# Two modulation vectors moved into the first feed-forward's second half, and an S5 input product with exchanged operands

## The chip, the cores and the metric

The kernel runs on one core of one Trainium2 chip. The metric is device time in microseconds (us) of one execution. Before the change three executions took 1390.58, 1391.0 and 1392.18 us; the median is 1391.0 us.

## The reference, cut to what matters

One inference step of a two-layer trunk (width 1024), for a prompt of 512 tokens and 8 samples of one token. All data are fp32. Layer 0 has an "even" mixer (gated linear attention beside RG-LRU), layer 1 an "odd" mixer (S5 beside HGRN2), and each mixer is followed by a SwiGLU feed-forward of inner width 2816. Every mixer and feed-forward is modulated from a condition vector:

```
mod = silu(c) @ w_ada[l] + b_ada[l]            # 6 vectors of 1024 for each layer
sh_m, sc_m, gt_m, sh_f, sc_f, gt_f = split(mod, 6)
h = x * (1 + sc_m) + sh_m;  x = LN(ALPHA*x + (1 + gt_m) * mixer(h))
h = x * (1 + sc_f) + sh_f;  x = LN(ALPHA*x + (1 + gt_f) * swiglu(h))
```

The two vectors that the change moves are sh_f and sc_f of layer 1, vectors 3 and 4: they are used right after the odd mixer. The S5 part of the odd mixer is evaluated in blocks of 8 tokens. For that, 32 groups of small matrices are prepared from parameters alone; one of them is, for each group g, a product of BA[g] (128 contraction rows by 128 columns, 8 powers by 16 inputs) with CS[g] (128 by 16 outputs).

## The kernel before, in words

**Order of the work.** The program goes through the even mixer, feed-forward 0 (lines 780 to 886, in two halves of 11 column blocks, `hb` 0 and 1), the odd mixer (from line 1647 on), feed-forward 1. Weights stream from DRAM in an order written out by hand, the list `plan` (lines 279 to 291). Each entry is one load of up to 1 MB into one of three raw buffers (`wraw`, line 45), issued on SP's queue at line 176. An entry that is a weight for the main products is used as one or two units of 128 columns; for each, `make` (line 181) has ACT cast it to fp32r (`whi`, line 199) and DVE subtract the remainder (`wlo`, line 110), and a raw buffer is free again when the remainder of its last unit is done. A main product (`mm3`, lines 231 to 241) takes 48 matmuls of 260 columns for 8 contraction blocks.

**The modulation entries.** An entry of kind "ada" holds two contraction blocks of w_ada for a vector of 1024, 1 MB. `ada_part` (line 319) does 8 plain fp32 matmuls with it, at four column positions of the array: the condition (128 by 32) is the stationary operand and 256 columns of the weight are the moving one (line 323). Four parts make a vector; then `ada_rows` (line 326) copies the sum to SBUF on ACT (`adasb`, line 328), transposes it with two matmuls (line 147) and adds the bias on DVE. The parts of a vector share one of the four PSUM buffers `mx`. `mix` puts "ada" entries between others: `FB` (vectors 1 and 2 of layer 1, 8 entries) in pairs into the second half of feed-forward 0, and `OA` (vectors 3 and 4, 8 entries) one by one among the 10 input-projection entries of the odd mixer, read from `od_in`.

**The odd mixer's start.** The layer norm at the end of feed-forward 0 is worked in two halves of the tokens (lines 660 to 770). The first five units of the input projection are worked for each half as it comes (`first_units`, matmuls of lines 816 to 818). Units 0 to 3 give `u`. They are copied by ACT into `ut` (line 1671), stored to DRAM (`Ud`, line 1675, and `Usd`, line 1695), and read back in another layout into `u8` (lines 1697 to 1699, ten loads of short runs), all of it on SP's queue. The S5 product `s5_in` (line 1716) needs the whole of `u8`. After it come the other units, the seven levels of HGRN2's chunk products (`level`, matmuls of lines 924 and 944, with DVE updating the operands between them), the S5 output and the output projection.

**S5's preparation.** `s5_prep` (from line 1440 on) runs as a side job in the first half of feed-forward 0: after each unit of the input projection it goes on by one step. Its last part goes through four chunks of 8 groups. DVE builds BA in three operations, eight matmuls transpose it (line 147), ACT copies that to `sb` (line 1615), which goes to DRAM; eight plain fp32 matmuls (line 1620) make the product with BA as the stationary operand and 16 columns of CS as the moving one; ACT copies it to `Mall` (line 1622). DVE's next work on this (CA and W of the same chunk, and BA of the next) takes buffers from a ring of four with the tag "W", so that it can wait for line 1620.

The order of the instructions on each engine is set when the program is built, by a scheduler that works with a simulated time line, priorities and free buffers; the engines then run it in order.

Of the kernel before, what the change touches and what calls it, by code (L numbers as in the profile page):

```python
# [7 lines left out]
F32 = mybir.dt.float32  # L8
# [28 lines left out]
OD_COLS = [0, 256, 1024, 1280, 512, 768, 1536, 1792, 2048, 2304]  # L37


def build(tc, I, O):  # L40
    nc = tc.nc
    V, S, G, T, SY = nc.vector, nc.scalar, nc.gpsimd, nc.tensor, nc.sync
    with ExitStack() as ctx:
        def pool(n, b=1, **k):
            return ctx.enter_context(tc.tile_pool(name=n, bufs=b, **k))
# [5 lines left out]
        tmp = pool("tmp", 6)  # L51
# [14 lines left out]
        def mx():  # L66
            return ps["M"].tile([128, 512], F32, tag="mx", name="mx")
# [41 lines left out]
        def tt(out, a, b, op):  # L109
            V.tensor_tensor(out=out, in0=a, in1=b, op=op)  # L110

        def add(out, a, b):
            tt(out, a, b, ALU.add)
# [16 lines left out]
        def bc(ap, shape):  # L130
            return ap.to_broadcast(shape)
# [13 lines left out]
        def transpose(out, in_, base=0):  # L145
            k = in_.shape[0]
            T.transpose(out, in_, ident[base:base + k, base:base + k])  # L147

        plan = []
# [94 lines left out]
        od_in, od_out = I["od_w_in"][0], I["od_w_out"][0]  # L244
# [3 lines left out]
        def p_ada(l, js):  # L248
            return [("ada", I["w_ada"][l], k0, 2, D * j, D, l) for j in js for k0 in range(0, 8, 2)]

        def p_cols(kind, src, cols):
            return [(kind, src, 0, 8, c, 256) for c in cols]

        def p_ffn(l, hb):
            r = []
            for c in range(0, 11, 2):
                n = min(2, 11 - c) * 128
                c0 = (11 * hb + c) * 128
                r.append(("fin", f_in[l], 0, 8, c0, n))
                r.append(("fin", f_in[l], 0, 8, DFF + c0, n))  # L260
            for cs in ((0,), (256,), (512, 768)) if hb else ((0,), (256,), (512,), (768,)):
                r += [("fout", f_out[l], 11 * hb + 8, 3, c0, 256) for c0 in cs]
                r += [("fout", f_out[l], 11 * hb, 8, c0, 256) for c0 in cs]
            return r

        def mix(main, ada, first=1, per=2):
            r = list(main[:first])
            rest = main[first:]
            done = 0
            for n, c in enumerate(rest):  # L270
                want = (n + 1) * (len(ada) // per) // len(rest) * per
                r += ada[done:want]
                done = want
                r.append(c)
            return r

        FA = p_ada(0, [5]) + p_ada(1, [0])
        FB = p_ada(1, [1, 2])
        OA = p_ada(1, [3, 4])
# [3 lines left out]
        plan += mix(p_cols("in", ev_in, EV_COLS), p_ada(0, range(2, 4)))  # L283
        plan += mix(p_cols("out", ev_out, (0, 256)), p_ada(0, [4])[:2], 1) + p_ada(0, [4])[2:] + p_cols("out", ev_out, (512, 768))
        plan += mix(p_ffn(0, 0)[:12], FA[:4], 3) + mix(p_ffn(0, 0)[12:], FA[4:])
        plan += mix(p_ffn(0, 1)[:-4], FB, 2) + p_ffn(0, 1)[-4:]
        plan += mix(p_cols("in", od_in, OD_COLS), OA, 0, 1)
        plan.append(("glu", I["od_s5_w_glu"][0], 0, 4, 0, 512))
        plan += p_cols("out", od_out, range(0, D, 256))
        plan += mix(p_ffn(1, 0)[:12], LA, 2, 1) + p_ffn(1, 0)[12:] + p_ffn(1, 1)  # L290
# [8 lines left out]
        h = (lambda k: hhi[:, k], lambda k: hlo[:, k])  # L299
# [9 lines left out]
        def ada_mm(p, r):  # L309
            for k in range(8):  # L310
                c = k % 4
                T.matmul(p[32 * c:32 * c + 32, 0:256], condT[:, k, :], r[:, k, :],
                         start=(k < 4), stop=(k >= 4), tile_position=(0, 32 * c), skip_group_check=True)
            sb = cst.tile([128, 256], F32, tag="adasb", name="adasb")
            S.copy(sb, p[:, 0:256])
            for b in range(2):
                T.matmul(p[:, 256 + 16 * b:256 + 16 * b + 9], sb[:, 128 * b:128 * b + 128], sel, start=True, stop=True)
            return p[:, 256:288].rearrange("p (c r) -> p c r", r=16)[:, :, 0:9]
# [54 lines left out]
        with tc.tile_pool(name="st", bufs=1, reuse_waits="tile") as st:  # L373
# [73 lines left out]
            for f in range(8):  # L447
# [5 lines left out]
                with tc.high_priority(offset=2 * HIGH):  # L453
                    q = ada_mm(mx(), r)
# [13 lines left out]
                for k in lag[f]:  # L468
                    for hf in range(2):
                        T.matmul(lrp[rows[hf], :HN], wl[:, k, :], h32s[k][:, hf], start=(k == 0),  # L470
                                 stop=(k == 7), tile_position=(0, 32 * hf), skip_group_check=True)
# [966 lines left out]
        def s5_prep(sp):  # L1438
            if True:
# [3 lines left out]
                def wt(nm, sh, parts=128):  # L1443
                    return sp.tile([parts] + sh, F32, tag="W", name=nm, bufs=4)
# [14 lines left out]
                for q in range(2):  # L1459
                    p = mx()  # L1460
# [11 lines left out]
                for n in range(2):  # L1472
                    p = mx()
# [122 lines left out]
                CS = tmp.tile([128, 32, 16], F32, tag="t2k", name="CS")  # L1596
                V.tensor_copy(CS[lo_], CT[0][lo_])
                ts1(CS[hi_], CT[1][hi_], -1.0, ALU.mult)
                Mall = wt("Mall", [512])
                for ch in range(4):  # L1600
                    gs = slice(8 * ch, 8 * ch + 8)
                    eb = lambda t: bc(t[:, :, gs].rearrange("p e g -> p g e").unsqueeze(3), [128, 8, 8, 16])
                    BA = wt("BA", [8, 8, 16])
                    W = wt("W", [8, 8, 16])
                    bb_ = lambda t: bc(t[:, :, gs].rearrange("p h g -> p g h").unsqueeze(2), [128, 8, 8, 16])
                    tt(BA, eb(XB), bb_(BT[0]), ALU.mult)
                    tt(W, eb(YB), bb_(BT[1]), ALU.mult)
                    add(BA, BA, W)
                    sb = wt("sb", [8, 128])
                    for q in range(2):  # L1610
                        p = mx()
                        for j in range(4):
                            g = 4 * q + j
                            transpose(p[:, j * 128:(j + 1) * 128], BA[:, g].rearrange("p e h -> p (e h)"))
                        S.copy(sb[:, 4 * q:4 * q + 4].rearrange("p a b -> p (a b)"), p)
                    G.dma_start(BATd[:, gs], sb)
                    pM = mx()
                    for g in range(8):
                        gg = 8 * ch + g
                        T.matmul(pM[:, g * 16:(g + 1) * 16], BA[:, g].rearrange("p e h -> p (e h)"), CS[:, gg],  # L1620
                                 start=True, stop=True)
                    S.copy(Mall[:, 128 * ch:128 * ch + 128], pM[:, 0:128])
                    yield
                    CA = wt("CA", [8, 8, 16])
                    W = wt("W", [8, 8, 16])
                    cb_ = lambda t: bc(t[:, gs].unsqueeze(2), [128, 8, 8, 16])
                    tt(CA, eb(XC), cb_(CT[0]), ALU.mult)
                    tt(W, eb(YC), cb_(CT[1]), ALU.mult)
                    add(CA, CA, W)
                    G.dma_start(CAd[:, gs], CA.rearrange("p g e h -> p g (e h)"))  # L1630
                    yield
# [350 lines left out]
        even_mixer()  # L1982

        ffn(0, s5_prep)
        odd_mixer()
        ffn(1)
# [31 lines left out]
```

## Time and profile before

| | |
|---|---|
| runs | 1390.58, 1391.0, 1392.18 us |
| profiled execution | 1391.37 us, of which the profile's span is 1389.4 us |
| TensorE busy | 1333.4 us, 96% of the span |
| VectorE busy | 764.9 us, 55% |
| ScalarE busy | 498.2 us, 36% |
| mean granted TensorE clock | 0.985 |
| read from DRAM | 167.11 MB |

In the rows, PE is TensorE, PEld its weight loads, DVE is VectorE, ACT is ScalarE, POOL is GpSimd, SP is SyncE and SPq its DMA queue. Durations of matmuls overlap, since matmuls are pipelined; what a group of them costs is read from the starts. A plain fp32 matmul leaves two records, a transposition one. The name behind "L" is a line of the kernel; a helper such as line 110 (a DVE operation on two tensors) or 147 (a transposition) serves many places.

### The profile page before, as it was taken

How to read it: one execution, taken by the hardware profiler on the slowest of the kernel's cores; microseconds unless marked ns; L12 is line 12 of the kernel's file. 1: busy time of each engine (PE TensorE's matmuls, PEld its weight loads, DVE VectorE, ACT ScalarE, POOL GpSimd, SP SyncE). 2: the span in 40 equal slices, each digit the busy share in tenths (PEclk: the TensorE clock that was granted, in tenths of full speed). 3: DMA queues.
4: the chain of work that ended last, by engine and by line, in shares of the span. 5: the costliest groups of instructions: out<-in, count | busy, mean ns of one | idle time of the engine just before them, and what ended most of it. 6: DMA issues, size and time to landing. Idle time of an engine off the chain costs nothing. (4 is left out here: it accounts for less than half of the span.)

```text
span 1389.4 us, 29467 instructions
## 1 busy us (share of the span) xinstructions
PE 1333.4 (96%) x12687; PEld 1267.0 (91%) x12687; DVE 764.9 (55%) x1726; ACT 498.2 (36%) x802; POOL 191.8 (14%) x215
## 2 busy tenths in 40 slices
PE   6998999989999999999998999999999999999996
PEld 4797988989998999999988999889899999999996
DVE  4677755687997233233592785566833233232365
ACT  3555536353232222222264123363533222222231
POOL 2200010340011200000170421013500000000013
PEclk9999999999999999999999999999999999999998
DMA  9643363413345842444458446432333323221211
GB/s 277 197 152 101 91 212 120 154 48 120 116 166 205 234 152 92 152 133 158 150 200 169 131 147 216 126 126 92 101 113 107 118 95 122 92 92 54 84 62 63
DMA packets 157628, 185.53 MB, mean 134 GB/s; under 512 B 18188, under 2 KB 137354, under 8 KB 157242
## 3 DMA queue, kind: packets, MB, share of 16 engines
q1 hardware_dynamic: 151514, 166.43, 38.7%
q0 software_dynamic: 5744, 17.08, 3.8%
q8 instruction: 100, 1.64, 0.5%
q14 instruction: 30, 0.25, 0.1%
q10 hardware_dynamic: 240, 0.13, 0.0%
HBM read 167.11 MB, written 15.36 MB: 131 GB/s over the span
## 5 line engine op out<-in xcount | busy, mean ns | idle before, releaser
L237 PE MATMUL acc<-hhi,whi 128*128 128x260 f32 x1936 | 398.8, 287 | 3.0 <-ACT whi L199 1.3
L199 ACT CAST whi<-raw 128x1024 fp32r<-128x1024 f32 (+2 forms) x198 | 187.7, 955 | 587.1 <-PE acc L239 428.1
L239 PE MATMUL acc<-hlo,whi 128*128 128x260 f32 x1936 | 396.2, 286 | 1.2 <-DVE hlo L110 1.2
L241 PE MATMUL acc<-hhi,wlo 128*128 128x260 f32 x1936 | 395.1, 285 | 0.0
L110 DVE TENSOR_TENSOR wlo<-raw,whi 128x1024 fp32r<-128x1024 f32 (+2 forms) x198 | 220.2, 1116 | 222.3 <-ACT whi L199 220.7
L237 PEld LDWEIGHTS acc<-hhi,whi 128*128 128x128 f32 x1936 | 300.5, 190 | 16.1 <-issue 5.9
L239 PEld LDWEIGHTS acc<-hlo,whi 128*128 128x128 f32 x1936 | 300.6, 190 | 4.4 <-DVE hlo L110 1.7
L241 PEld LDWEIGHTS acc<-hhi,wlo 128*128 128x128 f32 x1936 | 300.9, 190 | 2.3 <-issue 1.7
L239 PE MATMUL acc<-al,whi 128*128 128x260 f32 x576 | 116.0, 283 | 2.3 <-DVE al L110 2.3
L237 PE MATMUL acc<-ah,whi 128*128 128x260 f32 x576 | 116.4, 284 | 1.4 <-DVE x L122 0.8
L241 PE MATMUL acc<-ah,wlo 128*128 128x260 f32 x576 | 115.7, 283 | 0.0
L110 DVE TENSOR_TENSOR sg<-acc,sg 128x520 f32<-128x520 f32 (+1 forms) x48 | 31.0, 653 | 112.6 <-PE acc L241 108.1
L237 PEld LDWEIGHTS acc<-ah,whi 128*128 128x128 f32 x576 | 88.3, 188 | 4.8 <-ACT whi L199 2.3
L239 PEld LDWEIGHTS acc<-al,whi 128*128 128x128 f32 x576 | 88.6, 188 | 2.5 <-DVE al L110 2.5
L241 PEld LDWEIGHTS acc<-ah,wlo 128*128 128x128 f32 x576 | 88.6, 188 | 0.0
L524 POOL TENSOR_TENSOR s<-x 128x520 f32<-128x520 f32 x4 | 6.9, 1720 | 568.1 <-ACT whi L199 321.6
L110 DVE TENSOR_TENSOR smp<-acc,gt 128x8 f32<-128x8 f32 (+1 forms) x72 | 11.6, 161 | 119.0 <-PE acc L241 94.5
L816 PE MATMUL acc<-hhi,whi 128*128 128x260 f32 x208 | 59.2, 287 | 3.3 <-ACT hhi L774 3.3
L818 PE MATMUL acc<-hlo,whi 128*128 128x260 f32 x208 | 58.8, 289 | 3.3 <-DVE hlo L767 1.9
L817 PE MATMUL acc<-hhi,wlo 128*128 128x260 f32 x208 | 58.3, 282 | 0.0
L122 DVE SCALAR_TENSOR_TENSOR x<-acc,gt,x 128x512 f32<-128x512 f32 (+1 forms) x72 | 44.8, 622 | 0.0
L323 PE MATMUL mx<-raw,condT 128*32 128x256 f32 x640 | 44.2, 384 | 0.0
(592 smaller groups left out, 2017.5 us busy)
## 6 DMA issues: line engine op xcount, KB each, us to landing
raw<-in_w_ada_dram SPq DMA_DIRECT2D x40, 1024.0 KB, 6.1
raw<-in_ffn_w_in_dram SPq DMA_DIRECT2D x40, 1024.0 KB, 5.2
raw<-in_ffn_w_out_dram SPq DMA_DIRECT2D x16, 1024.0 KB, 5.3
raw<-in_ev_w_in_dram SPq DMA_DIRECT2D x10, 1024.0 KB, 9.4
raw<-in_od_w_in_dram SPq DMA_DIRECT2D x10, 1024.0 KB, 5.9
raw<-in_w_ada_dram SPq DMA_DIRECT2D x16, 512.0 KB, 7.3
raw<-in_ffn_w_out_dram SPq DMA_DIRECT2D x16, 384.0 KB, 3.1
raw<-in_ev_w_out_dram SPq DMA_DIRECT2D x4, 1024.0 KB, 5.3
```

The lines of the kernel that those rows point to most:

```text
L110: V.tensor_tensor(out=out, in0=a, in1=b, op=op)
L122: V.scalar_tensor_tensor(out=out, in0=a, scalar=s, in1=b, op0=op0, op1=op1)
L199: S.copy(hi[:, :nk, :m], rj)
L237: T.matmul(acc[:, hf, :HN], wh[:, k - koff, :], ah(k)[:, hf, :], start=st, stop=False)
L239: T.matmul(acc[:, hf, :HN], wh[:, k - koff, :], al(k)[:, hf, :], start=False, stop=False)
L241: T.matmul(acc[:, hf, :HN], wl[:, k - koff, :], ah(k)[:, hf, :], start=False, stop=sp)
L323: T.matmul(p[32 * c:32 * c + 32, 0:256], condT[:, k0 + k, :], r[:, k, 256 * c:256 * c + 256], start=(k0 + k == 0), stop=(k0 + k == 7), til ...
L524: G.tensor_tensor(out=lnt["s1"], in0=x[:, 0] if m == 1 else lnt["s1"], in1=x[:, m], op=ALU.add)
L816: T.matmul(out, wh[:, k, :], ah(k)[:, hf, :], start=n == 0, stop=False)
L817: T.matmul(out, wl[:, k, :], ah(k)[:, hf, :], start=False, stop=False)
L818: T.matmul(out, wh[:, k, :], al(k)[:, hf, :], start=False, stop=n == len(ks) - 1)
```

## The change

The eight entries `OA` go from the odd mixer's input projection into the second half of feed-forward 0, in pairs among its weights. In S5's preparation, CS becomes the stationary operand (two groups side by side, 32 columns, at four column positions) and BA the moving one (128 columns); the sum of 128 by 256 is copied to SBUF, transposed by two matmuls, and the blocks on the diagonal are copied to `Mall` by two copies.

```diff
-        plan += mix(p_ffn(0, 1)[:-4], FB, 2) + p_ffn(0, 1)[-4:]
-        plan += mix(p_cols("in", od_in, OD_COLS), OA, 0, 1)
+        plan += mix(p_ffn(0, 1)[:-4], FB + OA, 2) + p_ffn(0, 1)[-4:]
+        plan += p_cols("in", od_in, OD_COLS)
...
                     for g in range(8):
-                        gg = 8 * ch + g
-                        T.matmul(pM[:, g * 16:(g + 1) * 16], BA[:, g].rearrange("p e h -> p (e h)"), CS[:, gg],
-                                 start=True, stop=True)
-                    S.copy(Mall[:, 128 * ch:128 * ch + 128], pM[:, 0:128])
+                        c, gg = g % 4, 8 * ch + g - g % 2
+                        T.matmul(pM[32 * c:32 * c + 32, 128 * (g // 4):128 * (g // 4) + 128],
+                                 CS[:, gg:gg + 2].rearrange("p a b -> p (a b)"), BA[:, g].rearrange("p e h -> p (e h)"),
+                                 start=g < 4, stop=True, tile_position=(0, 32 * c), skip_group_check=True)
+                    mt = tmp.tile([128, 256], F32, tag="t2k", name="mt")
+                    S.copy(mt, pM[:, 0:256])
+                    for q in range(2):
+                        transpose(pM[:, 256 + 128 * q:384 + 128 * q], mt[:, 128 * q:128 * q + 128])
+                    mv = Mall[:, 128 * ch:128 * ch + 128].rearrange("p (a b h) -> p a b h", b=2, h=16)
+                    for b in range(2):
+                        S.copy(mv[:, :, b], pM[:, 256:512].rearrange("p (a b d h) -> p a b d h", b=2, d=2, h=16)[:, :, b, b])
```

## Rows read from the trace of the kernel before

**Rows 1.** The page's first part: busy time of TensorE, share of the span, instructions.
```profile
PE 1333.4 (96%) x12687; PEld 1267.0 (91%) x12687; DVE 764.9 (55%) x1726; ACT 498.2 (36%) x802; POOL 191.8 (14%) x215
```
**Rows 2.** Busy time of the engines in stretches (start and end in us, length, then busy us of PE, PEld, DVE, ACT, POOL; after them the granted clock as a share of full speed, the DMA engines' busy share and the GB/s they moved).
```profile
470.00:480.00 10.00, 10.00 (x85) 10.00 (x85) 3.06 (x6) 3.69 (x5) 2.36 (x2) 1.00 0.92 277
...
490.00:665.00 175.00, 175.00 (x1517) 170.27 (x1514) 56.18 (x79) 45.83 (x62) 1.32 (x2) 1.00 0.43 139
...
700.00:725.00 25.00, 22.07 (x190) 18.70 (x188) 24.52 (x68) 16.01 (x31) 16.48 (x16) 1.00 0.57 189
...
760.00:770.00 10.00, 4.06 (x53) 3.90 (x53) 1.81 (x7) 0.21 (x1) 0.97 (x2) 0.73 1.01 167
770.00:780.00 10.00, 10.00 (x112) 9.79 (x112) 7.40 (x24) 1.77 (x3) 5.34 (x7) 0.93 0.26 85
```
**Rows 3.** TensorE in order of time (start and duration in us) at the start of the odd mixer: its parts, and its waits.
```profile
711.06 1.50 PE L323 MATMUL mx<-raw,condT 128*32 128x256 f32 x24
...
722.54 1.07 PE L323 MATMUL mx<-raw,condT 128*32 128x256 f32 x16
725.08 0.36 PE L816 MATMUL acc<-hhi,wx 128*128 128x260 f32 x1 [1.47 <-DVE u_s L1673]
...
765.98 3.18 PE L1716 MATMUL mx<-u,bt 128*64 128x72 f32 x48 [5.94 <-DMA u<-Usd]
...
773.55 1.78 PE L1716 MATMUL mx<-u,bt 128*64 128x72 f32 x48
```
**Rows 4.** SP's queue in order of time there.
```profile
741.68 0.38 SPq L176 DMA_DIRECT2D raw<-in_od_w_in_dram  x1
742.40 0.34 SPq L1675 DMA_DIRECT2D Ud<-ut  x1
742.83 0.46 SPq L1695 DMA_DIRECT2D Usd<-u_s  x1
744.31 1.34 SPq L176 DMA_DIRECT2D raw<-in_w_ada_dram  x1
751.15 7.47 SPq L1697 DMA_DIRECT2D u<-Ud  x8
```
**Rows 5.** TensorE in order of time in the second half of feed-forward 0: a pair of parts, and later the two transpositions of a vector.
```profile
559.16 0.40 PE L239 MATMUL acc<-hlo,whi 128*128 128x260 f32 x2
559.40 0.40 PE L241 MATMUL acc<-hhi,wlo 128*128 128x260 f32 x2
559.73 1.93 PE L323 MATMUL mx<-raw,condT 128*32 128x256 f32 x32
561.59 0.51 PE L237 MATMUL acc<-hhi,whi 128*128 128x260 f32 x2
...
601.20 0.28 PE L237 MATMUL acc<-hhi,whi 128*128 128x260 f32 x1
601.32 0.38 PE L147 MATMUL mx<-ident,adasb 128*128 128x128 f32 x2
...
601.67 0.41 PE L239 MATMUL acc<-hlo,whi 128*128 128x260 f32 x2
```
**Rows 6.** TensorE in order of time around the first S5 chunk's product, and one level of HGRN2.
```profile
391.80 0.41 PE L239 MATMUL acc<-hlo,whi 128*128 128x260 f32 x2
392.05 1.85 PE L1620 MATMUL mx<-CS,BA 128*128 128x16 f32 x16
393.75 0.48 PE L241 MATMUL acc<-hhi,wlo 128*128 128x260 f32 x2
...
811.47 1.30 PE L924 MATMUL mx<-Qs,U 128*32 128x32 f32 x128
```
**Rows 7.** DVE and TensorE in order of time around the third and fourth S5 chunk and the end of the first half's input projection; in brackets the idle time before, and what ended it, as in rows 3.
```profile
424.38 1.23 DVE L110 TENSOR_TENSOR W<-YC,CT 128x1024 f32<-128x1024 f32 x1 [2.50 <-PE mx L1620]
...
430.42 2.02 DVE L110 TENSOR_TENSOR W<-YB,BT 128x1024 f32<-128x1024 f32 x1 [0.77 <-ACT ah L336]
...
434.23 0.39 PE L239 MATMUL acc<-al,whi 128*128 128x260 f32 x1 [2.33 <-DVE al L110]
```
**Rows 8.** ACT in order of time: a copy of 128x256 out of PSUM, and a cast of a 1 MB entry's unit that waited for its load.
```profile
419.02 0.37 ACT L328 COPY adasb<-mx 128x256 f32<-128x256 f32 x1 [0.35 <-PE mx L323]
...
652.11 1.06 ACT L199 CAST whi<-raw 128x1024 fp32r<-128x1024 f32 x1 [3.53 <-DMA raw<-in_ffn_w_out_dram]
```
**Rows 9.** Busy time in stretches, as in rows 2, for the matmuls of line 323 alone (PE busy, PEld busy, clock, DMA); 16 records are one part.
```profile
490.00:665.00 175.00, 8.11 (x132) 3.65 (x128) 1.00 0.43 139
700.00:725.00 25.00, 3.21 (x48) 1.25 (x48) 1.00 0.57 189
725.00:766.00 41.00, 1.68 (x16) 0.53 (x16) 0.98 0.89 194
766.00:900.00 134.00, 4.28 (x64) 1.67 (x64) 0.97 0.52 155
```
**Rows 10.** DMA issues from 735 to 770 us: count, size of each, and the median us from issue to landing; under them the four stores of `ut`, least, median and longest.
```profile
raw<-in_w_ada_dram SPq DMA_DIRECT2D x1, 1024.0 KB, 10.8
Usd<-u_s SPq DMA_DIRECT2D x1, 16.0 KB, 8.5
...
DMA to landing us min/median/max: 2.3/5.5/8.6
```
**Rows 11.** TensorE's wait between the levels, in order of time.
```profile
819.83 1.29 PE L924 MATMUL mx<-Qs,U 128*32 128x32 f32 x128 [0.73 <-DVE U L110]
```

## The prediction, made before the change was run

> **What bounds the kernel now.** I read first the page's part on busy time: TensorE is busy for 96% of the span [rows 1], so the time is TensorE's work plus its few waits, and a change is worth what it takes from either in its own stage. Next I read the busy time by stretches. The stretch that receives the eight parts has no idle TensorE time at all: 175.00 us of 175 us [rows 2]. What is added there is paid in full. The stretch that loses them is different: from 700 to 725 us TensorE is idle for 2.9 us while DVE is busy for 24.52 of 25 us, and in the ten microseconds from 760 us TensorE works for 4.06 us only, at a clock of 0.73 [rows 2]. Then the order of time there shows the one large wait, 5.94 us before the S5 input product, for the last load of u8 [rows 3]; and SP's queue shows what that load hangs on [rows 4].
>
> The change has two parts that touch at no buffer, so their terms are added.
>
> **Part 1, S5's product.** Before, one chunk's product starts at 392.05 us and the main product goes on at 393.75 us; its neighbour two matmuls earlier started at 391.80, and such neighbours lie 0.24 us apart [rows 5, 6], so it displaces 393.75 - 392.04 = 1.71 us, with a first pair of matmuls that lasts 0.48 instead of 0.41 us: 1.78 us. The new form isn't in the trace. Its nearest rows have the same stationary shape, 32 columns at four column positions: a pair of parts makes 16 products of 256 columns in 561.59 - 559.73 = 1.86 us, 0.116 us each [rows 5], and a level of HGRN2 64 products of 32 columns (128 records, two each) in 1.30 us, 0.020 us each [rows 6]. For 128 columns the line between them gives 0.020 + 0.096 x 96/224 = 0.061 us, so 0.49 us for the eight; the bounds are 0.16 and 0.93 us. To that comes the change of shape: the pair of parts pushes the main product from 559.64 to 561.59 and makes its first two matmuls 0.10 us longer, 2.05 us for 1.86 us of parts, so 0.19 us. The two new transpositions cost 0.23 us, as those of a vector do: from 601.20 to 601.67 instead of 0.24 us [rows 5]. New sum 0.91 us, saving 0.87 us for a chunk and 3.5 us for four; by the bounds 1.7 to 4.8 us.
>
> What could take this back is DVE: TensorE waits 2.33 us for a remainder (al) at 434.23 us, which DVE makes only after a 2.02 us operation of the fourth chunk [rows 7]. But DVE's chunk work itself stood still for 2.50 us until the third product was done [rows 7], so a faster product moves DVE's chain forward as well. I keep -3.5 us, and 0 as the other end. On ACT a chunk gets a copy of 128x256 (0.37 us, [rows 8]) and two smaller ones, at most 1.1 us together, against the copy that it loses; ACT is busy for 36% of the span [rows 1]. If ACT is late, the two transpositions stand in TensorE's queue with the main product behind them; the scheduler puts other matmuls ahead of them, as it does for a vector [rows 5]. Nobody waits early for Mall, which is used when all chunks are done. The new buffer in the ring of six is held for one copy and two transpositions. Cost of these: nothing, else part of the 3.5 us.
>
> **Part 2, what feed-forward 0 gains in work.** Eight parts cost 8 x 2.05/2 = 8.2 us (the eight already there: 8.11 us busy, [rows 9]), two vectors' transpositions 2 x 0.23 us: +8.7 us. Their copies and the bias additions lie on ACT and DVE, busy for 46 and 56 of 175 us [rows 2]. The loads: 8 MB more in this stretch, which moves 139 GB/s; with them (139 x 175 + 8400)/184 = 178 GB/s, and 277 GB/s was moved with TensorE fully busy [rows 2]. So the mean is no limit, only a dense place: the last two pairs stand with one small output entry between them and a 1 MB entry behind them. Already before, the cast of that 1 MB entry waited 3.53 us for its load [rows 8]. With a pair more ahead of it, the load is issued after the pair's first part; the small entry's 4.3 us (36 matmuls at 0.12 us) and the second pair's 2.05 us then cover most of its issue to landing and cast. I take +0.5 us, between 0 and 2.5 us.
>
> **Part 2, what the odd mixer loses.** Line 323 is busy there for 3.21, 1.68 and 4.28 us in three stretches [rows 9].
>
> *700 to 725 us.* Three parts stand in the layer norm's shadow: DVE is the bound, and after the third TensorE waits 1.47 us for DVE all the same [rows 2, 3]. Of 3.2 us I take -1.0 us, between 0 and -3.2 us.
>
> *725 to 766 us.* The part here (1.68 us, in two pieces) stands after u's last matmuls, so taking it away only lets TensorE come earlier to the wait. What ends the wait is the chain on SP's queue: the last store of u at 742.40 us and the store of the samples at 742.83 us, then a wait for their landing, the ten loads from 751.15 us on, and the product at 765.98 us [rows 3, 4]. The ten loads stay. The landing took 8.6 us, where the quickest store took 2.3 and the median 5.5 us [rows 10]. Beside it run a 1 MB weight load issued at 741.68 us, which keeps its place (the next weight takes it), and a 1 MB load of w_ada issued at 744.31 us [rows 4], which goes. I take the median: 8.6 - 5.5 = 3.1 us earlier. The bounds are 0 and the whole of the wait. That forecasts a wait of 5.94 - 3.1 + 1.68 = 4.5 us still, and a product that starts 3.1 us earlier. The wait also lowers the clock: granted 0.73 and 0.93 of full speed in the two stretches [rows 2], and the first input product takes 3.18 us where the second takes 1.78 us [rows 3]: 1.4 us, and 0.07 x 10 = 0.7 us, together 2.1 us at the lower of the two levels. With a shorter wait I take a third of it, -0.7 us.
>
> The row on the landing times has w_ada's load behind the store in the queue and still before the landing. The Trainium skill (DMA: Bandwidth & Descriptors, Queues, rings and completion order) says that one queue's descriptors are consumed in ring order and that a completion comes only after the earlier writes of that DMA engine. By that rule a load issued 1.9 us after the store can't hold it back, and the term would be 0. The quickest store against the longest speaks for traffic as the cause, but not for which load. It is a rival below.
>
> *766 to 900 us.* Four parts, 4.28 us, and 2 x 0.23 us of transpositions stand in a stretch that TensorE bounds but for small waits. One of them stands just ahead of a level, where TensorE waits 0.73 us for DVE already [rows 11]; I count that one at a third: 4.7 - 0.7 = -4.0 us, between -2.3 us (half, if DVE sets the pace of the levels) and -4.7 us. The raw buffers and the PSUM buffer that the parts held come free for the odd mixer; I price that at nothing, since no row shows a wait for them alone.
>
> **Sum.** -3.5 + 8.7 + 0.5 - 1.0 - 3.1 - 0.7 - 4.0 = -3.1 us against the profiled execution's 1391.37 us (span 1389.4 us and 2.0 us around it): 1388.3 us. That execution lies 0.4 us above the median of the runs, so 1387.9 us.
>
> **The rivals.** *The wait doesn't move (slower).* The store lands when it did, for the queue's order, and the parts before 766 us were cover: terms 0, 0, 0 for the layer norm, the chain and the clock, and half of what follows, -2.3 us. Then -3.5 + 8.7 + 0.5 - 2.3 = +3.4 us: 1394.4 us. It decides where the wait before line 1716 grows from 5.94 us to 7 us or more. For it: the median of four stores is thin, and the rule cited above. Against: the three loads in flight together.
>
> *The wait goes almost wholly.* The stores land in the 2.3 us of the quickest and the loads, without w_ada's ahead of them, run faster: the chain gives all of 5.94 us and the clock 2.1 us, 8.0 instead of 3.8 us: 1383.7 us. For it: w_ada's load needs 10.8 us to land, beyond the first of the ten loads [rows 4, 10]. Against: those ten have short runs and take most of the time.
>
> *The exchange of operands does nothing for the time*, because the wait for DVE at 434 us takes back what TensorE gains, or the transpositions wait for ACT: 3.5 us more, 1391.4 us.
>
> **How the numbers follow.** The forecast's case gets 0.40, the wait that stays 0.22, the wait that goes 0.18, the exchange without effect 0.15, and 0.05 is left for an order of the scheduler that none of these describes. A measurement of this kernel can tell 0.2%, 2.8 us, from no change: the borders are 1388.2 and 1393.8 us. The forecast lies just beyond the lower one, and its terms are loose by some us, so of its 0.40 I count 0.24 as faster and 0.16 as same; the wait that goes is faster (0.18), the exchange without effect same (0.15, of which 0.03 goes to slower with a starved load in the dense place), the wait that stays slower. With the rest: faster 0.44, same 0.31, slower 0.25. The likeliest case alone spans 1385 to 1391 us. The range reaches to the other two cases and a little beyond on either side, for the bounds of the dense place and of the layer norm: 1382.5 to 1395.0 us.
>
> **What would show it.** Right: line 1620's group of a chunk displaces about 0.9 us with its transpositions; line 323 is busy for 16 us in feed-forward 0's second half, which is 8 to 10 us longer; no w_ada load stands in SP's queue in the odd mixer; the wait before line 1716 is 3 to 5 us, and the stores of u land in about 5.5 us. Wrong: a wait there of 7 us or more or below 2 us, casts that wait for loads between the last pairs with TensorE idle, a wait for al beyond 4 us, or an odd mixer whose levels wait longer for DVE.

## The result, and the profile after

The change made the kernel slower. After it the median is 1401.22 us (1399.89 to 1404.99), before it 1390.79 us (four executions each); the ratio is 1.0082, with a 95% interval of 1.0062 to 1.0102. The forecast was 1387.9 us, with a range up to 1395.0 us: the direction was wrong, and the time lies outside the range. The profiled execution took 1400.65 us, with a span of 1398.9 us against 1389.4 us: 9.5 us to account for.

The first part of the page after the change, which answers to [rows 1]:

```profile
PE 1335.6 (95%) x12695; PEld 1270.8 (91%) x12695; DVE 761.6 (54%) x1726; ACT 498.7 (36%) x810; POOL 188.6 (13%) x215
```

TensorE's busy time grew by 2.2 us only, so most of the 9.5 us is new idle time. To find its place I cut both spans at the same matmuls, by the starts of TensorE's rows (us): the transposition that ends feed-forward 0's first half (492.97 before, 491.40 after), the first matmul of the layer norm's statistics (694.50, 706.36), the first one that uses the second half's samples (725.08, 736.92), and the first S5 input product (765.98, 778.69).

| stage | before | after | difference | forecast |
|---|---|---|---|---|
| to the end of feed-forward 0's first half | 492.97 | 491.40 | -1.6 | -3.5 |
| feed-forward 0's second half | 201.53 | 214.96 | +13.4 | +9.2 |
| layer norm, first units of the first half | 30.58 | 30.56 | 0.0 | -1.0 |
| first units of the second half, up to the S5 product | 40.90 | 41.77 | +0.9 | -3.1 |
| from the S5 product to the end | 623.42 | 620.21 | -3.2 | -4.7 |

(The forecast's clock term of -0.7 us is put to the last row.) Every stage came out worse than forecast.

**Feed-forward 0's second half.** Busy time by stretches, as in [rows 2]: the stretch from 490 us on, and two in the dense place at its end.

```profile
490.00:665.00 175.00, 174.70 (x1574) 165.92 (x1573) 52.67 (x72) 42.91 (x57) 1.29 (x1) 1.00 0.52 173
660.00:670.00 10.00, 7.45 (x69) 6.30 (x69) 2.52 (x3) 2.67 (x4) 0.00 (x0) 0.87 0.79 272
670.00:680.00 10.00, 10.00 (x82) 10.00 (x82) 3.49 (x8) 1.16 (x2) 1.49 (x1) 0.96 0.46 154
```

The same for line 323 alone, which answers to [rows 9]:

```profile
490.00:665.00 175.00, 15.47 (x256) 7.50 (x256) 1.00 0.52 173
```

All 16 parts stand in the feed-forward now (256 records, 16 a part) and none in the odd mixer. The stretch up to 665 us is full, as forecast; the ten microseconds from 660 us are not. TensorE in order of time there (start, duration; in brackets the idle time before and what ended it), and under it ACT and then SP's queue:

```profile
663.02 1.93 PE L323 MATMUL mx<-raw,condT 128*32 128x256 f32 x32
667.50 0.80 PE L237 MATMUL acc<-ah,whi 128*128 128x260 f32 x2 [2.55 <-ACT whi L199]
```

```profile
666.40 1.99 ACT L199 CAST whi<-raw 128x1024 fp32r<-128x1024 f32 x2 [8.09 <-DMA raw<-in_ffn_w_out_dram]
```

```profile
657.77 0.37 SPq L176 DMA_DIRECT2D raw<-in_w_ada_dram  x1
658.63 11.60 SPq L176 DMA_DIRECT2D raw<-in_ffn_w_out_dram  x4
```

The 1 MB load of w_ffn_out is behind the last w_ada load in the queue; ACT stands idle for 8.09 us until it is there, and TensorE for 2.55 us. The two matmuls after the wait take 0.80 us, twice the 0.40 us of such a pair [rows 5]: the granted clock of the two stretches is 0.87 and 0.96.

**The odd mixer's start.** Busy time by stretches from the layer norm to the S5 product:

```profile
710.00:730.00 20.00, 18.52 (x133) 17.87 (x132) 19.93 (x50) 12.05 (x21) 13.77 (x15) 0.91 0.61 209
730.00:740.00 10.00, 6.18 (x40) 6.00 (x40) 8.02 (x28) 7.09 (x15) 6.28 (x8) 0.78 0.01 2
740.00:750.00 10.00, 10.00 (x77) 10.00 (x76) 2.70 (x9) 2.47 (x4) 2.13 (x2) 0.88 0.00 0
770.00:780.00 10.00, 2.81 (x35) 2.63 (x35) 0.91 (x1) 3.00 (x5) 0.00 (x0) 0.83 1.39 152
```

TensorE in order of time, which answers to [rows 3]: the last matmuls before the wait for the second half, those after it, and the S5 product.

```profile
732.70 0.28 PE L817 MATMUL acc<-hhi,wx 128*128 128x260 f32 x1
732.82 0.28 PE L818 MATMUL acc<-hlo,wx 128*128 128x260 f32 x1
736.92 0.56 PE L816 MATMUL acc<-hhi,wx 128*128 128x260 f32 x1 [3.82 <-DVE u_s L1680]
...
739.44 0.42 PE L818 MATMUL acc<-hlo,wx 128*128 128x260 f32 x1
739.66 0.42 PE L816 MATMUL acc<-hhi,wx 128*128 128x260 f32 x1
...
778.69 4.14 PE L1723 MATMUL mx<-u,bt 128*64 128x72 f32 x64 [7.19 <-DMA u<-Ud]
```

Two things are to be seen. The three parts that left the layer norm, 3.2 us of work, left a hole: the wait grew from 1.47 us [rows 3] to 3.82 us, and the stage is as long as before. (The clock, 0.91 in the stretch from 710 to 730 us, is enough for the rest of the 3.2 us.) And the hole has a tail: ahead of it neighbouring matmuls start 0.12 us apart, after it 0.22 us apart, until 742.3 us. That is the lower of the two clock levels (1.2 instead of 2.4 GHz) for 5.4 us, some 25 starts at 0.1 us more each, 2.4 us. The wait before the S5 product grew too, from 5.94 us [rows 3] to 7.19 us. Also, the trace has 263 main matmuls of 260 columns between the second half's first and the S5 product, where there were 274: 11 x 0.12 = 1.3 us of work went behind the product. This makes the stage's sum: -1.7 for the part, -1.3, +1.25 for the wait, +2.4 for the clock are +0.7 us, and +0.9 was measured. Behind the product, -4.7 us for four parts with their transpositions and +1.3 are -3.4 us, and -3.2 was measured. The product itself runs at the lower level as it did before: 4.14 us for 64 records and 3.18 us for 48 [rows 3], 0.065 us a record. SP's queue, which answers to [rows 4]:

```profile
755.97 0.38 SPq L176 DMA_DIRECT2D raw<-in_od_w_in_dram  x1
756.70 1.04 SPq L1682 DMA_DIRECT2D Ud<-ut  x1
757.83 1.69 SPq L1702 DMA_DIRECT2D Usd<-u_s  x1
765.69 5.27 SPq L1704 DMA_DIRECT2D u<-Ud  x8
```

No w_ada load is behind the stores any more, and yet the first load of u8 goes out 9.0 us after the last store of u, against 8.75 us [rows 4].

**S5's preparation.** (The product whose operands were exchanged stands here, at line 1620; it is not the S5 input product of the odd mixer, for all that the title says.) TensorE in order of time around the first chunk, which answers to [rows 6], and the wait that answers to [rows 7]:

```profile
392.13 0.41 PE L239 MATMUL acc<-hlo,whi 128*128 128x260 f32 x2
392.47 0.64 PE L1620 MATMUL mx<-BA,CS 128*32 128x128 f32 x16
393.04 0.51 PE L241 MATMUL acc<-hhi,wlo 128*128 128x260 f32 x2
...
432.05 0.80 PE L239 MATMUL acc<-al,whi 128*128 128x260 f32 x2 [2.82 <-DVE al L110]
```

The eight products move the main product from 392.37 to 393.04 us, 0.67 us, with a first pair 0.1 us longer, and the two transpositions, at 395.91 us, take 0.2 us: 1.0 us against the 1.78 us of before. DVE's wait for the third chunk's product, 2.50 us [rows 7], is 0.20 us, and al comes some 2 us earlier; TensorE is there earlier still and waits 2.82 us for al instead of 2.33 us.

The end of this stage shows what became of the gain. From the first chunk's product to the end of the half it was 100.92 us before and is 98.93 us now. In the last but one kernel of the experiments, which has the same exchange and the same plan up to here, it is 97.30 us, 3.6 us less than before. The two differ behind the wait for al: from there to the half's end it is 59.35 us in after and 57.93 us in that kernel. Busy time around the wait, in after and then in that kernel; the clock, 0.84 and 1.00, stands third from the end:

```profile
425.00:435.00 10.00, 7.18 (x49) 6.97 (x48) 8.66 (x8) 3.26 (x6) 0.53 (x1) 0.84 0.35 133
```

```profile
425.00:435.00 10.00, 7.22 (x73) 6.83 (x71) 9.11 (x8) 2.66 (x5) 0.00 (x0) 1.00 0.27 83
```

### The profile page after: what moved, and what is told of

Its sections match the earlier page's. It is cut to its first block, busy times and chain, and to the rows that moved or that the text cites. A ratio compares the mean times of both kernels' runs of the same rounds, so it can differ in the third digit from the quotient of the medians.

```text
span 1398.9 us, 29497 instructions
## 1 busy us (share of the span) xinstructions
PE 1335.6 (95%) x12695; PEld 1270.8 (91%) x12695; DVE 761.6 (54%) x1726; ACT 498.7 (36%) x810; POOL 188.6 (13%) x215
## 5 line engine op out<-in xcount | busy, mean ns | idle before, releaser
L237 PEld LDWEIGHTS acc<-hhi,whi 128*128 128x128 f32 x1936 | 299.1, 189 | 15.5 <-issue 5.7
L816 PEld LDWEIGHTS acc<-hhi,whi 128*128 128x128 f32 x208 | 40.6, 196 | 4.4 <-ACT hhi L774 3.8
```

Of the source, the lines that this page charges most:

```text
L237: T.matmul(acc[:, hf, :HN], wh[:, k - koff, :], ah(k)[:, hf, :], start=st, stop=False)
L816: T.matmul(out, wh[:, k, :], ah(k)[:, hf, :], start=n == 0, stop=False)
```

## The experiments

The theories: **cover**, that the parts of the odd mixer's start stood in TensorE's waits for DVE and for u8, so that taking them away gives nothing and the longer waits lower the clock besides; the **dense place**, that the feed-forward pays for the last pairs of parts more than their work; and the **queue**, that u's stores land late for what stands ahead of them in SP's queue, not for the w_ada load behind. The rival to each is the forecast's own step. "after" is the changed kernel; ratios are to the kernel before, with 95% intervals. The experiments ran on two chips, where the kernel before had medians of 1388.28 us (the halves alone, the dense place, the first run with the stores on ACT's queue) and 1391.18 us (the others), so kernels are compared by their ratios; waits and stages are those of one profiled execution each.

**Each half of the change alone.** First the exchange of operands, with the plan as before:

```diff
-        plan += mix(p_ffn(0, 1)[:-4], FB + OA, 2) + p_ffn(0, 1)[-4:]
-        plan += p_cols("in", od_in, OD_COLS)
+        plan += mix(p_ffn(0, 1)[:-4], FB, 2) + p_ffn(0, 1)[-4:]
+        plan += mix(p_cols("in", od_in, OD_COLS), OA, 0, 1)
```

Expected: 

> Part 1 alone (exchanged operands; the modulation entries as before). Theory, from the trace of the changed kernel (its last part of feed-forward 0's first half ends 1.57 us earlier than before although it began 0.3 us later): the exchange saves about 2 us, 1388 to 1390 us, and the whole loss comes from the move. Rival: the exchange made the wait for the remainder at the end of the first half longer (2.82 instead of 2.33 us) and pulled the clock down there; then it is no faster than before, 1391 us or more.

Measured: 0.9990 (0.9976 to 1.0005), 1388.28 us, not to be told from no change; the span is 1386.7 us. Feed-forward 0's first half ends at 491.32 us instead of 492.97 us: -1.65 us. TensorE's wait for al is there again, 2.81 us.

Then the plan's change, in the kernel before:

```diff
-        plan += mix(p_ffn(0, 1)[:-4], FB, 2) + p_ffn(0, 1)[-4:]
-        plan += mix(p_cols("in", od_in, OD_COLS), OA, 0, 1)
+        plan += mix(p_ffn(0, 1)[:-4], FB + OA, 2) + p_ffn(0, 1)[-4:]
+        plan += p_cols("in", od_in, OD_COLS)
```

Expected: 

> Part 2 alone (the eight modulation entries moved, S5's product as before). Theory: the move alone costs 11 to 12 us, 1402 to 1403 us: 8.7 us of work and about 4 us of waits and slow clock in the second half of feed-forward 0, against 2 to 4 us that the odd mixer gives back. Rival: the loss comes from the two edits together (another order of the scheduler); then this kernel is within 4 us of before.

Measured: 1.0112 (1.0082 to 1.0141), 1404.15 us, somewhat more than expected. The whole loss is the move's.

**The dense place.** All pairs stand among the first ten entries of the second half, so that no pair comes just ahead of the output weights:

```diff
-        plan += mix(p_ffn(0, 1)[:-4], FB + OA, 2) + p_ffn(0, 1)[-4:]
+        plan += mix(p_ffn(0, 1)[:10], FB + OA, 2) + p_ffn(0, 1)[10:]
```

Expected: 

> The changed kernel with all eight pairs put among the first ten entries of feed-forward 0's second half, none near its small output entries. Theory: the wait of 2.55 us at its end goes, with the slow clock behind it: 3 to 4 us less than the changed kernel, 1397 to 1398 us, and the stretch is still longer than before by the 8.7 us of work. Rival (the loads are too many for the stretch as a whole): a wait of that size comes back between the dense pairs, and the time stays at 1401 us.

Measured: 1.0046 (1.0027 to 1.0065), 1394.84 us, better than expected (the profiled execution was one of its longer ones, 1398.37 us). Feed-forward 0's second half takes 210.22 us, which is 8.69 us more than the 201.53 us before, and 209.69 us in two later kernels with the same placing: the forecast's price of the work, 8.7 us, is met within half a us, and the dense place is the other 5 of the 13.4 us. Busy time by stretches in this kernel, as above:

```profile
660.00:670.00 10.00, 10.00 (x86) 10.00 (x85) 5.50 (x7) 3.26 (x4) 2.20 (x1) 1.00 0.31 102
```

What is left of the loss lies behind it. TensorE's two waits at the odd mixer's start (4.15 and 9.26 us) are, if anything, longer than in after:

```profile
732.32 0.56 PE L816 MATMUL acc<-hhi,wx 128*128 128x260 f32 x1 [4.15 <-DVE u_s L1680]
...
775.04 4.13 PE L1723 MATMUL mx<-u,bt 128*64 128x72 f32 x64 [9.26 <-DMA u<-Usd]
```

**Cover, kept.** Four of the eight parts go back to the odd mixer, all of them ahead of the S5 product; the other four stay in the feed-forward, with no dense place:

```diff
-        plan += mix(p_ffn(0, 1)[:10], FB + OA, 2) + p_ffn(0, 1)[10:]
-        plan += p_cols("in", od_in, OD_COLS)
+        plan += mix(p_ffn(0, 1)[:10], FB + OA[:4], 2) + p_ffn(0, 1)[10:]
+        od = p_cols("in", od_in, OD_COLS)
+        plan += od[:1] + OA[4:5] + od[1:2] + OA[5:6] + od[2:3] + OA[6:7] + od[3:4] + OA[7:8] + od[4:]
```

Expected: 

> Exchanged operands; only one vector is moved (four parts, as two pairs more among the first ten entries of feed-forward 0's second half), the other's four parts stay in the odd mixer at the first four places, as before. Theory (the parts before the S5 input product were cover for waits, the ones behind it were work): the four that move cost 4.3 us there and give 4.7 us back behind the S5 input product, so the time is that of the exchange alone, ratio to before 0.997 to 1.001. Rival (moved work is lost work wherever it stood, because every part costs the feed-forward more than it gives back): about half of the loss of the kernel with all eight moved, ratio 1.002 to 1.004.

Measured: 1.0023 (1.0008 to 1.0038), 1392.48 us, above what was expected and inside the rival's range. The cover works: the wait in the layer norm is 1.58 us, that before the S5 product 5.2 us, both as with no part moved (1.42 and 4.46 us with the exchange alone, 1.47 and 5.94 us before), and from the product to the end it is 3.7 us less than with the exchange alone. But the feed-forward's half takes 209.53 us, 8.0 us more than before for 4.3 us of added work, with one wait of its own that none of the other kernels has (lines behind the plan stand one further down here), and a clock of 0.83 in the ten microseconds from 620 us:

```profile
621.25 0.44 PE L147 MATMUL mx<-ident,adasb 128*128 128x128 f32 x2 [2.40 <-ACT adasb L329]
```

Without that wait and the clock behind it the account would come out within 2 us of the exchange alone, as the theory has it, but the ratio by itself does not tell theory and rival apart. The next kernel does.

**Cover, added.** The kernel without the dense place, with four of its parts computed once more at the odd mixer's start:

```diff
-        plan += p_cols("in", od_in, OD_COLS)
+        od = p_cols("in", od_in, OD_COLS)
+        plan += od[:1] + OA[0:1] + od[1:2] + OA[1:2] + od[2:3] + OA[2:3] + od[3:4] + OA[3:4] + od[4:]
```

Expected: 

> All eight moved as in the kernel with no pair in the dense place, and the first four computed a second time in the odd mixer, at the first four places (the same values are written again): 4.3 us of TensorE work and 4 MB of loads more. Theory (cover): the wait before the second token half falls from 4.15 to about 1.5 us, the granted clock stays at 1.00 there, and the time is no longer than without the added work, ratio 1.002 to 1.005 where that kernel had 1.0046. Rival (the parts cost their work wherever they stand): 4.3 us more, ratio 1.0077.

Measured: 1.0009 (0.9997 to 1.0022), 1391.74 us, a smaller ratio than expected. With some 4.3 us more of matmuls and 4 MB more of loads, the kernel is faster than the one it is made from: the ratios lie 0.37% apart, 5 us, and their intervals just do not meet. TensorE in order of time: three parts' records ahead of the second half's units (line 324 here), the two waits, and the S5 product.

```profile
718.26 1.50 PE L324 MATMUL mx<-raw,condT 128*32 128x256 f32 x24
...
720.33 0.64 PE L324 MATMUL mx<-raw,condT 128*32 128x256 f32 x8
...
729.78 1.07 PE L324 MATMUL mx<-raw,condT 128*32 128x256 f32 x16
731.62 0.36 PE L817 MATMUL acc<-hhi,wx 128*128 128x260 f32 x1 [0.77 <-DVE u_s L1681]
...
771.11 3.17 PE L1724 MATMUL mx<-u,bt 128*64 128x72 f32 x48 [4.52 <-DMA u<-Usd]
```

Its stretches from 720 us on, to be read against those of after from 730 us on:

```profile
720.00:730.00 10.00, 10.00 (x86) 9.07 (x88) 9.37 (x27) 6.69 (x12) 7.26 (x7) 1.00 0.74 253
730.00:740.00 10.00, 9.23 (x86) 8.67 (x79) 6.07 (x18) 4.42 (x10) 5.88 (x6) 1.00 0.58 211
740.00:750.00 10.00, 10.00 (x87) 9.26 (x85) 4.05 (x7) 5.34 (x7) 0.00 (x0) 1.00 0.61 189
```

The layer norm's stage is 30.95 us, with three parts more in it, and 30.96 us without them: that work costs nothing. Behind it the clock is granted in full where the kernel without cover has 0.83 (730 to 740 us); the stage up to the S5 product is 39.49 us instead of 42.72 us, although it holds one part and eleven main matmuls (274 instead of 263) more; from there to the end it is 618.69 instead of 621.36 us, of which those eleven explain 1.3 us. So a part there is not merely free: it is worth something, since it keeps the wait short and the clock up.

**u's stores on ACT's queue.** The stores leave SP's queue, where the 1 MB loads are; in the traces, TensorE's and GpSimd's order stays as it was, and DVE's but for a small operation or two. In after:

```diff
-                        SY.dma_start(Ud[m], ut[:, m])
+                        S.dma_start(Ud[m], ut[:, m])
...
-                SY.dma_start(Usd.rearrange("m p b -> p m b"), u_s)
+                S.dma_start(Usd.rearrange("m p b -> p m b"), u_s)
```

Expected: 

> The changed kernel with u's stores (four of ut, one of the samples) issued on ACT's queue in place of SP's; TensorE's and DVE's order are the same. Theory (the store lands late because it stands in SP's ring behind a 1 MB weight load issued 0.7 us earlier): the last store lands in 2 to 4 us instead of 8.7, the first load of u8 is issued 4 to 6 us earlier, and the wait before the S5 input product falls from 7.2 to 2 or 3 us; with the clock 4 to 7 us less, 1395 to 1397 us. Rival (the landing is slow because all queues share the DMA engines with the weight load): the landing stays at 7 to 9 us and so does the time, 1400 to 1402 us.

Measured: 1.0072 (1.0049 to 1.0096), 1397.84 us; the expected gain does not show in the time, which can't be told from after's 1.0082. In the stage itself it does show. From the last store of u to the first load of u8 it is 6.1 us instead of 9.0 us, and the wait before the product 3.79 us instead of 7.19 us. The queues and the product in this kernel:

```profile
757.14 0.33 ACTq L1682 DMA_DIRECT2D Ud<-ut  x1
757.59 0.82 ACTq L1702 DMA_DIRECT2D Usd<-u_s  x1
```

```profile
756.41 0.38 SPq L176 DMA_DIRECT2D raw<-in_od_w_in_dram  x1
763.27 5.17 SPq L1704 DMA_DIRECT2D u<-Ud  x8
```

```profile
775.73 3.75 PE L1723 MATMUL mx<-u,bt 128*64 128x72 f32 x64 [3.79 <-DMA u<-Ud]
```

The stage up to the product is 4.3 us shorter (37.43 instead of 41.77 us). But from the product to the end this execution takes 623.86 us and after's 620.18 us, with TensorE's order the same; most of that is the clock, which is granted to 0.77 in this stretch and to 0.94 in after:

```profile
895.00:925.00 30.00, 26.15 (x148) 23.32 (x148) 21.28 (x61) 11.33 (x15) 6.66 (x10) 0.77 0.40 126
```

In all ten traces the clock is at its lower level for a while near 890 to 920 us, in some four times as long as in others; one execution of each kernel doesn't tell whether the edit has a part in that.

So moving the stores saves some 3 us of the landing, and 6 us stay. The DMA packets show what those are. q1 is SP's queue and q10 ACT's; packets, MB and share of the 16 engines from 758.2 to 761.0 us, behind the last store's issue at 757.14 us, and from 761.0 to 763.0 us:

```profile
q1 hardware_dynamic: 751, 0.77, 93.7%
q10 hardware_dynamic: 8, 0.01, 1.8%
...
q10 hardware_dynamic: 672, 0.28, 49.1%
q1 hardware_dynamic: 189, 0.18, 25.7%
```

The last store and the samples (0.28 MB) move only when the 1 MB load issued 0.7 us ahead of the store has nearly ended, although it is in another queue. What is gone is a tail: in after, with all of it in SP's queue, the last 0.21 MB took from 762.0 to 765.5 us, with the engines busy for a fifth:

```profile
q1 hardware_dynamic: 405, 0.21, 19.7%
```

The same edit in the kernel without the dense place:

Expected: 

> The kernel with no pair in the dense place, with u's stores on ACT's queue; the same order on TensorE and DVE. Theory: the two are separate losses and add up: the wait before the S5 input product falls from 9.3 us by 3 us or more, ratio 1.0015 to 1.003 where the one had 1.0046, still not below before, since the feed-forward keeps 8.7 us of added work. Rival: the wait is set by the ten loads of u8 alone, ratio 1.0046 again.

Measured: 1.0016 (1.0000 to 1.0031), 1391.85 us, as expected; store to load 6.1 us, wait 4.38 us. The dense place and the tail of the stores are mended here, the longer wait in the layer norm (4.17 us) and the work added to the feed-forward are not, and the kernel is level with the one before, not ahead of it.

**The best of them.** The exchange of operands with the plan as before, and u's stores on ACT's queue (the edits of the first and of the sixth experiment):

Expected: 

> The exchange alone, with u's stores on ACT's queue in place of SP's; TensorE, DVE and POOL have the same order as with the exchange alone. Theory (the stores wait in SP's ring behind weight loads): the last store lands 3 us earlier and the wait before the S5 input product falls from 4.5 to 1 or 2 us: 1384 to 1386 us where before has 1388.3, ratio 0.996 to 0.998, so that this is below both kernels. Rival (w_ada's load, issued right behind the stores, shares the DMA engines with them on any queue): the landing and the time stay, ratio 0.999.

Measured: 0.9946 (0.9926 to 0.9966), 1382.41 us (four executions), which beats both kernels, and by more than expected. TensorE's row of the S5 product, and the stretches around it:

```profile
759.69 1.75 PE L1723 MATMUL mx<-u,bt 128*64 128x72 f32 x48 [1.75 <-DMA u<-Usd]
```

```profile
750.00:760.00 10.00, 8.25 (x75) 8.07 (x76) 2.48 (x6) 6.67 (x10) 0.00 (x0) 1.00 1.39 134
760.00:770.00 10.00, 10.00 (x150) 9.71 (x146) 7.90 (x24) 1.55 (x2) 5.26 (x6) 1.00 0.55 167
```

The wait is 1.75 us, the clock stays at 1.00 and the product's 48 records take 1.75 us, where the kernel with the exchange alone waits 4.46 us and takes 3.17 us for them. The gain in the span, 5.0 us (1386.7 to 1381.7), is 2.7 us of wait, 1.4 us in the product itself, 0.6 us in what follows it, and 0.3 us ahead of that stage.

## Why the prediction was wrong

The forecast missed by 12.6 us (-3.1 us against +9.5 us in the span): 4.2 us in feed-forward 0's second half, 4.0 us in the stage up to the S5 product, 1.9 us in S5's preparation, 1.5 us behind the product and 1.0 us in the layer norm. By its own steps, with what each measured:

- **Part 1, S5's product** (-3.5 us, bounds 1.7 to 4.8): the mechanism was right; -1.6 us was measured in the stage, -1.65 us with the exchange alone. The products' own gain was nearly as worked out, 0.8 instead of 0.87 us for a chunk (the eight took 0.57 instead of 0.49 us), and DVE's chain did move forward. What took back some 1.5 us is a term that the forecast put at nothing: the clock behind the wait for al. Where it stays full, in the two traces with the exchange that have it so, the stretch from the first product on gives 3.3 and 3.6 us. The exchange need not be its cause: in the trace of the move alone, which has the old product and a wait of 2.35 us, the clock falls there too, and from that wait to the half's end it is 60.24 instead of 58.74 us. The other 0.4 us went ahead of the first product, where the exchange has no part.
- **The work in feed-forward 0** (+8.7 us): right within half a us, by the kernels without the dense place (+8.2 to +8.7 us).
- **The dense place** (+0.5 us, bounds 0 to 2.5): wrong, about +5 us. The idle time alone is at the upper bound (2.55 us); I let the small entry and the second pair cover the load, and the load took 8.09 us of ACT's time. What was not in the bounds at all is the clock after the wait (0.87 and 0.96) and three small waits of 0.25, 0.76 and 0.64 us, where before had one of 0.84 us.
- **The layer norm** (-1.0 us, bounds 0 to -3.2): wrong, 0.0 us. DVE bounds that stage, and I had read this from the row (24.52 of 25 us, [rows 2]); a third of the parts' time was a compromise between two answers, and the row allowed one only.
- **725 to 766 us, the chain of u** (-3.1 us): the step whose mechanism failed. I put the long landing on the w_ada load behind the store. Without that load, store to first load of u8 took 9.0 us (after) and 9.7 us (the kernel without the dense place); with it 8.75 us (before), 8.7 us (exchange alone) and 8.5 us (cover added): the load behind did not hold the store back. The rule cited from the Trainium skill (DMA: Bandwidth & Descriptors, Queues, rings and completion order) said so, and these runs agree with it. The 1 MB weight load ahead of the store does hold it back: on ACT's queue it took 5.9 to 6.1 us in three kernels, and there too the store's packets came only when that load's were nearly done. The trace of before could have told. The median of 5.5 us is not one of four stores, as I took it, but the middle of the two whose landing was recorded, 2.3 and 8.6 us. And the quick one had a 1 MB load 0.44 us behind it, which did not hold it back, and no load in SP's queue for 12 us ahead of it. Both rows of SP's queue, and that store's time to landing in us, at the end of its line:

```profile
736.19 0.34 SPq L1675 DMA_DIRECT2D Ud<-ut  x1
736.63 0.38 SPq L176 DMA_DIRECT2D raw<-in_od_w_in_dram  x1
...
Ud<-ut SPq DMA_DIRECT2D x1, 256.0 KB, 2.3
```

- **The clock** (-0.7 us): wrong in sign. At the product nothing changed (0.065 us a record before and after); a second spell at the lower level appeared that I had not thought of, behind the layer norm's wait, +2.4 us. I had priced the clock at the one wait that I hoped to shorten, and not at those that a removed part would lengthen, nor at the one for al and the one in the dense place.
- **766 to 900 us** (-4.0 us, bounds -2.3 to -4.7): right. The gain was -3.2 us from the product to the end, and -4.5 us without the 1.3 us of other work that came behind the product. Where cover was added it was -5.3 us against the exchange alone (618.69 and 624.01 us), which is 0.6 us more than the work that went.

The rival on the slower side had the right mechanism, with a wait of over 7 us as its sign (7.19 us was measured), and gave 1394.4 us. It fell short by what it shared with the forecast, the S5 term and the dense place, and by the clock, for which it took 0. My chances leaned to the forecast since I set a count of loads in flight against the order of the queue, and the forecast took all of its gain in this stage on that count.

Left open: why the load and the store behind it end in a slow tail when both are in SP's queue, and why the lower clock level lasts longer in some traces than in others.

## What to carry to other kernels

Before work is moved out of a stage, look at what ends the next wait there: where it is another engine's chain or a DMA, the work was cover: its removal gave nothing here, and the stage that received it paid in full. Price each wait that grows at more than its own length, since the granted clock can be at the lower level for some microseconds behind it. A store that something waits for is worth trying on a queue that has no large load ahead of it: that one edit was worth 0.4% with the exchange alone (ratios of 0.9990 and 0.9946) and 0.3% without the dense place, against 0.1% for the exchange; in the changed kernel its gain can't be told.

## What was not expected of the hardware

- A wait of 3.82 us, after 20 us in which TensorE was busy for 18.52 us, was followed by 5.4 us at the lower clock level (0.22 us between matmuls instead of 0.12 us), while behind the wait of 1.47 us in the same place [rows 3] the matmuls from 725.08 us on started 0.12 us apart. The ten traces divide the same way: five with parts in the layer norm wait 0.77 to 1.58 us there and keep the full clock behind it, five without wait 3.82 to 4.17 us and have the lower level for 3 to 6 us behind it. Adding 4.3 us of matmuls that nobody needs brought the clock back to 1.00 and made the kernel some 5 us faster.
- With a 1 MB load 0.7 us ahead in SP's queue, 8.4 to 9.7 us passed from the issue of a 256 KB store there to the first load that depends on it (seven kernels); with the store on ACT's queue it was 5.9 to 6.1 us (three kernels), and its packets still came behind that load's.
- Plain fp32 products with 32 stationary columns at four column positions and 128 moving columns took 0.57 us for eight, 0.07 us each, where the line through its nearest shapes gave 0.06 us.
